# A decoder step's mixer: the scan's columns projected earlier, side steps priced in VectorE time, four raw weight buffers

## Chip, cores and metric

The kernel runs on one core of a Trainium2 chip. The metric is device time in microseconds (us) of one execution; the time before is the median of three runs. The profile is that of one further execution, and its own time stands in the table below.

## The reference

One layer of a decoder step for 256 prompt tokens, 16 learned meta tokens and 8 x 4 sample tokens, all in float32, model width 2048:

```
x = x + 1/2 * SwiGLU_1(rms(x))
[u_a | u_b | g_a | g_b] = rms(x) @ W_in
a = PoolMix(u_a)          # causal means over 2, 4, 8, 16 tokens, minus identity,
                          # a 256x256 map per group, a scale per channel
b = GLU(gelu(S5(u_b)))    # diagonal complex recurrence, 64 groups of 64 states
x = x + (sig(g_a) * (a @ W_a) + sig(g_b) * (b @ W_b)) @ W_out
x = x + 1/2 * SwiGLU_2(rms(x))
y = rms(x)
```

The last pooling inputs and the final S5 states are outputs too.

## The kernel before

Tokens are columns: 304 of them (`NT`) up to the mixer's first half, 288 (`NL`) once the meta tokens are dropped. Channels are partitions, in tiles of 128. Every product is made of three matmuls, because a float32 operand is split into a high and a low part in the faster type `fp32r`: high by high, high by low, low by high (`mm3`, lines 249 to 254).

All weights come in chunks of 512 x 256 in one fixed order, `weight_order`. For each chunk the load queue of SyncE fetches `raw` (L138), ScalarE casts its high part `whi` (L161) and VectorE subtracts to get the low part `wlo` (L172). There are `RAW = 3` raw buffers, and `AHEAD + 2 = 4` each for the two parts.

`proj` multiplies one chunk in 24 matmuls and then calls `step`. A `step` makes the high part of a later chunk, flushes `g.post` (work that reads finished PSUM banks), makes the low part, starts a load, and then takes some side steps: `g.owed` grows by `g.rate`, and for each whole unit one item is drawn from the generator `g.side`. All engines run their instructions in the order in which this program issues them, so the rate decides how much side work stands between two weight splits on VectorE.

Before the mixer the side work is the preparation of the S5 tables (`ssm_setup`, at `SETRATE`). In the mixer it is the pooling (`Pool.run`, at `POOLRATE = 3.5` items a step) and then the scan (`Scan.run`, at `MIXRATE = 1.53` items a step).

The mixer goes through these stages. First the eight column pairs of `W_in` for the two branches, in the order `COLS = (0, 1, 2, 4, 3, 5, 6, 7)`: 0 to 3 feed the pool, 4 to 7 the scan. Pair 0 is projected ahead of the mixer, while the norm's scale is still being worked out. Then come the pool's group maps (`mixed`), the eight pairs of the first gate with `w_branch_a` (6 steps each), the eight pairs of the second gate (4 steps each), the GLU, `w_branch_b` and `w_out`.

The scan has eight matrices `i`, each in two halves. One half is eight `rows` on VectorE (L965, L966, L949 with L951, two scans L955, L971, L959, L962). Between the rows the generator issues, at hand-written places: `into` (matmuls `bu` for the next matrix, copied by ScalarE), `outof` (24 matmuls `yps` for the matrix before, two rows into the next one), the pieces of `act` (gelu, on ScalarE and VectorE in turn), and the transfers of GpSimd's queue: `load` (`ee` from `esc`), `stored` and `stacked` (an input split, written to `usc` and read back as `us`), and `matrices` (`bs`, `cs`). `Scan.first` and `Scan.begin` do this for the first matrix, around and within the projection of pair 5. Before the scan's generator starts, `drain` issues all that is left of the pool.

The names that the change touches: `RAW`, `MIXRATE`, `POOLRATE`, `COLS`, `LAG`, `MIXLAG`; `step`, `also`, `drain`; `Scan.input`, `stored`, `into`, `outof`, `rows`, `run`; `Pool.run`, `means`; `mixer`.

Of the kernel before, what the change touches and what calls it, by code (L numbers as in the profile page):

```python
# [33 lines left out]
AHEAD = 2  # L34
RAW = 3
SETRATE = 1.25
MIXRATE = 1.53
WP = 1024
# [8 lines left out]
NCON = NT + NTV + 2  # L47
POOLRATE = 3.5
LATE = 8
STIR = 7  # L50
LAG = 0
MIXLAG = 2
COLS = (0, 1, 2, 4, 3, 5, 6, 7)
MAGIC = 12582912.0
# [128 lines left out]
def setup(ctx, tc, I):  # L183
    g = Ctx()
    nc = tc.nc
    g.tc, g.nc, g.I = tc, nc, I
    g.uid = 0
    g.side, g.rate, g.owed, g.post = None, 0, 0.0, []
    g.dram = ctx.enter_context(tc.tile_pool(name="dram", bufs=1, space=DRAM))
    g.const = ctx.enter_context(tc.tile_pool(name="const", bufs=1))  # L190
    g.w = Weights(g, ctx.enter_context(tc.tile_pool(name="wpool", bufs=2)))
    g.act = ctx.enter_context(tc.tile_pool(name="act", bufs=1))
    g.parts = {"X": (g.act, 2 * KD)}
    g.psum = ctx.enter_context(tc.tile_pool(name="psum", bufs=4, space=PSUM))
    g.psaux = ctx.enter_context(tc.tile_pool(name="psaux", bufs=3, space=PSUM))
    g.pslong = ctx.enter_context(tc.tile_pool(name="pslong", bufs=1, space=PSUM))
    g.downs = 0

    g.ones = g.const.tile([P, P], F32, name="ones")
    nc.vector.memset(g.ones, 1.0)  # L200
    g.vec = g.const.tile([P, NVEC], F32, name="vec")
    return g
# [17 lines left out]
def step(g):  # L220

    g.w.high()
    flush(g)
    g.w.low()
    g.w.load()
    g.owed += g.rate
    while g.owed >= 1.0:
        g.owed -= 1.0
        got = next(g.side, None) if g.side is not None else None
        if got is None:  # L230
            g.side = None

# [7 lines left out]
def also(g, more):  # L240
    g.side = more if g.side is None else chain(g.side, more)


def drain(g):
    while g.side is not None:
        if next(g.side, None) is None:
            g.side = None

# [590 lines left out]


class Scan:

# [8 lines left out]
    def input(self, ps, r):  # L851

        u = self.sp.tile([P, NT], F32, name=nm(self.g, "u"))
        self.g.nc.vector.tensor_tensor(u, ps, r, ALU.mult)
        self.u.append(u)
        if len(self.u) == 1:
            self.stored(0)
            self.stacked(0)
# [17 lines left out]
    def stored(self, i):  # L876

        g, nc = self.g, self.g.nc
        hi = self.sp.tile([P, NT], F32R, tag="uhi", name=nm(g, "uhi"), bufs=1)
        lo = self.sp.tile([P, NT], F32R, tag="ulo", name=nm(g, "ulo"), bufs=1)  # L880
        nc.scalar.copy(hi, self.u[i])
        nc.vector.tensor_tensor(lo, self.u[i], hi.bitcast(F32), ALU.subtract)
        for k, u in enumerate((hi, lo)):
            nc.gpsimd.dma_start(g.usc[i][k], u)
# [8 lines left out]
    def into(self, i, pair, ri, half, long=False):  # L893

        g = self.g
        if "row" not in pair[half]:
            pair[half]["row"] = self.sp.tile([P, 3, JB, NT], F32, tag="row", name=nm(g, "row"), bufs=4)
        row = pair[half]["row"][:, 1 + ri]
        for jj in range(JB):
            q = half * JB + jj  # L900
            ps = bank(g, "bu", aux=True, pool=g.pslong if long and jj else None)[:, :NT]
            g.nc.tensor.matmul(ps, self.bs[i][:, q, ri * P:(ri + 1) * P], self.up[:, q], start=True, stop=True)  # L902
            g.nc.scalar.copy(row[:, jj], ps)

    def outof(self, i, pair):
# [3 lines left out]
        c = self.cs[i].rearrange("p i (q c) -> p i q c", c=32)  # L909
        for k, h in enumerate((2, 1, 0)):  # L910
            for half, s in enumerate(pair):
                for jj in range(JB):
                    q = half * JB + jj
                    g.nc.tensor.matmul(self.yps[i][q * 32:q * 32 + 32], c[:, h, q], s["row"][:, h, jj, NMETA:],  # L914
                                       start=k == 0, stop=k == 2)

# [16 lines left out]
    def rows(self, sb, s):  # L933
# [23 lines left out]
        def back():  # L957
            x, e = (y.rearrange("p k j t -> p (k j) t")[:, :, NMETA:] for y in (row, ee))
            tt(x, x, e, ALU.mult)  # L959

        def states():
            tt(self.st[:, :, :, js].rearrange("p r k j -> p r j k"), both(one[:, :, S0 - 1::NS]),  # L962
               two[:, :, :, S0 - 1::NS], ALU.subtract)

        return [lambda: tt(fl(one), fl(two[:, 0]), fl(two[:, 1]), ALU.add),  # L965
                lambda: tt(row.rearrange("p k j t -> p (k j t)"), row.rearrange("p k j t -> p (k j t)"),  # L966
                           ee.rearrange("p k j t -> p (k j t)"), ALU.mult),
                turned,
                lambda: scan(2),
                lambda: scan(1),  # L970
                lambda: tt(one[:, :, NMETA:], two[:, 1, :, NMETA:], two[:, 0, :, NMETA:], ALU.add),  # L971
                back,
                states]

# [17 lines left out]
    def run(self):  # L992
# [4 lines left out]
        for i in range(KW):  # L997
            nxt = [{} for _ in range(half)]
            for h in range(half):
                sb = i * half + h  # L1000
                rows = self.rows(sb, pair[h])
                if sb >= 1 and sb + 1 < nb:
                    new = self.load(sb + 1)
                    (nxt[0] if h else pair[1])["ee"] = new["ee"]
                for n, row in enumerate(rows):
                    row()
                    if h == 0 and n == 2 and done is not None:
                        self.outof(i - 1, done)
                        acts = self.act(i - 1)
                    if h == 0 and n == 5 and i + 1 < KW:  # L1010
                        self.matrices(i + 1, ins=False)
                    k, late = divmod(h * len(rows) + n - 4, 3)
                    if i + 1 < KW and late == 0 and 0 <= k < 4:
                        self.into(i + 1, nxt, 1 - k % 2, k // 2)
                    if h == 0 and n == 1 and i + 2 < KW:
                        self.stored(i + 2)
                    if h and n == 6 and i + 2 < KW:
                        self.stacked(i + 2)
                        self.matrices(i + 2, outs=False)
                    while acts and h * len(rows) + n >= acts[0][0]:  # L1020
                        acts.pop(0)[1]()
                    yield 1
            done, pair = pair, nxt
        for _ in range(3):
            yield 1
        self.outof(KW - 1, done)
        yield 1
        for n, f in self.act(KW - 1):
            f()
            if n in (5, 7):  # L1030
                yield 1

# [5 lines left out]
class Pool:  # L1038


    def __init__(self, g, O):
# [9 lines left out]
        t2 = T()  # L1051
        self.f = [cut(t2, 0), cut(t2, 1)]
        self.LE = LE

# [3 lines left out]
    def run(self, p, pss, norm, out):  # L1058
# [6 lines left out]
        for u, end in zip(self.u, e):  # L1065
            nc.scalar.copy(end[:, :, HIST:], u[:, S0:].rearrange("p (b s) -> p b s", s=NS))
        yield 1
        for f in range(2):
# [4 lines left out]
    def means(self, w, u, e, out):  # L1073
# [4 lines left out]
        while k < w:  # L1078
# [3 lines left out]
            s, es, k, a = s2, e2, 2 * k, a ^ 1  # L1082
            yield 1
        stt(d[:, :NPR], s[:, NMETA:S0], 1.0 / w, u[:, NMETA:S0], ALU.mult, ALU.subtract)
        stt(d[:, NPR:].rearrange("p (b s) -> p b s", s=NS), es[:, :, HIST:], 1.0 / w, e[:, :, HIST:],
            ALU.mult, ALU.subtract)
        yield 1
        out.append(split(g, d, NL, "Y"))
        yield 1

# [7 lines left out]
def mixer(g, norm, O, ps0):  # L1098
# [8 lines left out]
    def gate(ps, c):  # L1107
        z = Z()[:, :NL]
        nc.vector.tensor_tensor(z, ps, norm.r[:, NMETA:], ALU.mult)
        nc.scalar.activation(z, z, AF.Sigmoid, bias=vcol(g, "b_gate", c))  # L1110
        return z

    with ExitStack() as cm:
        g.mix = cm.enter_context(g.tc.tile_pool(name="mix", bufs=1))
        with ExitStack() as cs:
# [3 lines left out]
            dparts, aparts = [], []  # L1119
            g.side, g.rate = None, POOLRATE  # L1120
            def spare(c):
                if c == KD // KC - 1:
                    g.owed -= MIXLAG

            for p in COLS:
                if p < KW // 2:
                    pool.fetch(p)
                before = {KW // 2 + 1: scan.begin, KW - 1: spare}.get(p)
                ps = proj(g, "w_in", p * 256, norm.x, NT, KD, before) if p else ps0
# [3 lines left out]
                else:  # L1133
                    g.post += [lambda q=q: scan.input(q, norm.r) for q in ps]
                if p == 1:
                    scan.first()
                if p == KW // 2 + 1:
                    drain(g)
                    g.side, g.rate = scan.run(), MIXRATE
                    g.owed = -LAG * MIXRATE  # L1140
            def mixed():
                g.owed -= MIXLAG
                for q in range(4):
# [4 lines left out]
                    for f in range(2):  # L1148
                        ps = bank(g, "pw")[:, :NL]
                        for k in range(2):  # L1150
# [3 lines left out]
                        g.post.append(lambda i=2 * q + f, ps=ps: aparts.append(  # L1154
                            split(g, ps, NL, "Y", vcol(g, "pool_scale", i))))
                    if q % 2:
                        step(g)

            mixed()
            for p in range(KD // 2):  # L1160
# [5 lines left out]
                def gated(p=p, z=z, pa=pa):  # L1166
                    for f in range(2):
                        nc.vector.tensor_tensor(z[f], pa[f], z[f], ALU.mult)
                        nc.sync.dma_start(msc[2 * p + f], z[f])

# [337 lines left out]
```

## Time and profile before

| what | value |
|---|---|
| median of three runs | 2317.06 us (2316.76 to 2318.68) |
| the profiled execution, its own time | 2318.77 us |
| its span, first to last instruction | 2316.8 us |
| granted TensorE clock, mean | 0.999 |
| mixer's first projection to the second gate's end | about 892 to 1285 us |
| weight traffic and all other DMA | 437.36 MB, mean 189 GB/s |

The span is what the engines' rows cover; some 2 us of the execution's time lie around it. Engines are named PE (TensorE matmul), PEld (its weight load), DVE (VectorE), ACT (ScalarE), POOL (GpSimd) and SP (SyncE). A row such as `wlo<-raw,whi` names the tile written and the tiles read, and `L172` the line of the kernel. Matmuls are pipelined: each is shown as about 0.3 us long while a new one starts every 0.13 to 0.14 us, so the count of matmuls in a stretch says more than the busy time.

### The profile page before, as it was taken

To read this page: it belongs to the slowest core of one execution; us is meant where nothing else is said; L and a number is where in the kernel's file an instruction comes from. 1 tells how busy PE (TensorE), PEld (TensorE's weight loads), DVE (VectorE), ACT (ScalarE), POOL (GpSimd) and SP (SyncE) were. 2 spreads that over 40 slices of the span, in tenths; PEclk is the share of its full clock that TensorE was granted. 3 is DMA by queue.
4 is the path that set the end of the run, shared out by engine and by line. 5 is a ranking of instruction groups with operands and counts; after the bars stand their busy time and mean duration, and the time that the engine had idled before them with its cause. 6 is when DMAs were issued, how large, how long until landed. Compare 5 with 4: busy or idle time off the path is not lost.

```text
span 2316.8 us, 41582 instructions
## 1 busy us (share of the span) xinstructions
PE 2306.3 (100%) x17073; PEld 2293.3 (99%) x17073; DVE 1576.1 (68%) x2303; ACT 942.9 (41%) x1316; POOL 134.8 (6%) x255
## 2 busy tenths in 40 slices
PE   9999999999999999999999999999999999999998
PEld 9999999999999999999999999999999999999998
DVE  7788777877654557799999765545555555555556
ACT  5333333343333335454444544433333333333333
POOL 0000000002200002211110130000000000000001
PEclk9999999999999999999999999999999999999999
DMA  6445555556654446767785775444444444444543
GB/s 230 160 151 188 197 209 205 189 202 212 203 174 160 156 155 214 238 220 246 258 265 199 235 264 175 163 167 162 172 164 166 167 168 164 164 165 166 169 159 128
DMA packets 133454, 437.36 MB, mean 189 GB/s; under 512 B 22064, under 2 KB 33632, under 8 KB 133136
## 3 DMA queue, kind: packets, MB, share of 16 engines
q1 hardware_dynamic: 107088, 375.51, 47.6%
q0 software_dynamic: 25792, 58.87, 8.4%
q8 instruction: 134, 2.20, 0.4%
q14 instruction: 56, 0.46, 0.1%
q10 hardware_dynamic: 384, 0.32, 0.0%
HBM read 403.07 MB, written 31.55 MB: 188 GB/s over the span
## 4 chain that ended last, share of the span: by engine, by line
PE 98%; DVE 1%; issue 0%; ACT 0%; DMA 0%; SPq 0%; ACTq 0%; DVEq 0%
PE pj L253 24%; PE pj L252 24%; PE pj L254 24%; PE dn L254 8%; PE dn L252 8%; PE dn L253 8%; PE yps L914 1%; PE bu L902 0%; DMA pk<-in_first 0%; PE o L1245 0%; DVE row L955 0%; DVE wlo L172 0%; PE pw L253 0%; PE pw L252 0%; PE pw L254 0%
## 5 line engine op out<-in xcount | busy, mean ns | idle before, releaser
L172 DVE TENSOR_TENSOR wlo<-raw,whi 128x1024 fp32r<-128x1024 f32 (+1 forms) x697 | 849.6, 1220 | 576.5 <-ACT whi L161 575.6
L161 ACT CAST whi<-raw 128x1024 fp32r<-128x1024 f32 (+1 forms) x697 | 729.1, 1048 | 1202.6 <-PE pj L253 690.7
L252 PE MATMUL pj<-X,whi 128*128 128x304 f32 (+1 forms) x2428 | 728.3, 300 | 0.7 <-ACT whi L151 0.7
L253 PE MATMUL pj<-X,whi 128*128 128x304 f32 (+1 forms) x2428 | 728.2, 300 | 0.0
L254 PE MATMUL pj<-X,wlo 128*128 128x304 f32 (+1 forms) x2428 | 727.8, 300 | 0.0
L253 PE MATMUL pj<-Y,whi 128*128 128x288 f32 x1728 | 510.6, 296 | 0.0
L252 PE MATMUL pj<-Y,whi 128*128 128x288 f32 x1728 | 509.4, 295 | 0.0
L254 PE MATMUL pj<-Y,wlo 128*128 128x288 f32 x1728 | 508.8, 294 | 0.0
L252 PEld LDWEIGHTS pj<-X,whi 128*128 128x128 f32 x2428 | 457.2, 188 | 4.0 <-issue 2.1
L253 PEld LDWEIGHTS pj<-X,whi 128*128 128x128 f32 x2428 | 456.6, 188 | 0.1
L254 PEld LDWEIGHTS pj<-X,wlo 128*128 128x128 f32 x2428 | 456.3, 188 | 0.2
L252 PEld LDWEIGHTS pj<-Y,whi 128*128 128x128 f32 x1728 | 325.1, 188 | 0.9 <-issue 0.5
L253 PEld LDWEIGHTS pj<-Y,whi 128*128 128x128 f32 x1728 | 324.9, 188 | 0.0
L254 PEld LDWEIGHTS pj<-Y,wlo 128*128 128x128 f32 x1728 | 324.6, 188 | 0.0
L254 PE MATMUL dn<-H,wlo 128*128 128x304 f32 x704 | 213.0, 303 | 0.0
L252 PE MATMUL dn<-H,whi 128*128 128x304 f32 x704 | 212.8, 302 | 0.0
L253 PE MATMUL dn<-H,whi 128*128 128x304 f32 x704 | 212.2, 301 | 0.0
L254 PE MATMUL dn<-X,wlo 128*128 128x288 f32 x688 | 203.0, 295 | 0.0
L253 PE MATMUL dn<-X,whi 128*128 128x288 f32 x688 | 203.0, 295 | 0.0
L252 PE MATMUL dn<-X,whi 128*128 128x288 f32 x688 | 202.7, 295 | 0.0
L253 PEld LDWEIGHTS dn<-H,whi 128*128 128x128 f32 x704 | 132.4, 188 | 0.0
L252 PEld LDWEIGHTS dn<-H,whi 128*128 128x128 f32 x704 | 132.3, 188 | 0.0
(278 smaller groups left out, 1816.5 us busy)
## 6 DMA issues: line engine op xcount, KB each, us to landing
raw<-in_ffn_w_gate SPq DMA_DIRECT2D x175, 512.0 KB, 3.3
raw<-in_ffn_w_up SPq DMA_DIRECT2D x175, 512.0 KB, 3.3
raw<-in_ffn_w_down SPq DMA_DIRECT2D x168, 512.0 KB, 3.3
raw<-in_w_in SPq DMA_DIRECT2D x96, 512.0 KB, 4.3
raw<-in_w_out SPq DMA_DIRECT2D x32, 512.0 KB, 3.9
esc<-ee POOLq DMA_DIRECT2D x16, 912.0 KB, 5.7
ee<-esc POOLq DMA_DIRECT2D x16, 912.0 KB, 5.9
raw<-in_w_branch_a SPq DMA_DIRECT2D x16, 512.0 KB, 4.2
```

The lines of the kernel that those rows point to most:

```text
L161: self.g.nc.scalar.copy(hi[:, :kn], self.raw[i][:, :kn])
L172: self.g.nc.vector.tensor_tensor(lo[:, :kn], raw[:, :kn], hi[:, :kn].bitcast(F32), ALU.subtract)
L252: mm(ps, wh, x[0], start=start, stop=False)
L253: mm(ps, wh, x[1], start=False, stop=False)
L254: mm(ps, wl, x[0], start=False, stop=stop)
L914: g.nc.tensor.matmul(self.yps[i][q * 32:q * 32 + 32], c[:, h, q], s["row"][:, h, jj, NMETA:], start=k == 0, stop=k == 2)
```

## The change

There are three parts.

The order: pairs 4 and 5, the scan's first, are projected second and fourth. The scan's generator starts after pair 5 as before, but without draining the pool: the pool now has a lane of its own, `g.front`, which is served ahead of `g.side`. The pool's result tiles are claimed when it is set up.

The pace: an item of a generator is no longer one unit. It yields VectorE's time for it in us, and `step` books that against `g.rate`, which is the time of a step (3.355 us with 304 columns, 3.186 with 288) less that of a weight split (1.135). Work that is issued outside the generators is booked too: inputs, gates and pool maps reduce `g.owed`, and the scan's own matmuls add to it, since they lengthen the step. The places of `into` in the row order are written as a list, and are the same as before. The switch `DIRECT` is empty, so the code that it chooses isn't used.

The buffers: `RAW` goes from 3 to 4.

```diff
-RAW = 3
+RAW = 4
 SETRATE = 1.25
-MIXRATE = 1.53
+LOWUS, SHORTUS, LONGUS = 1.135, 3.186, 3.355
+TIGHT = 0.0
...
-POOLRATE = 3.5
+DIRECT = ()
...
-COLS = (0, 1, 2, 4, 3, 5, 6, 7)
+COLS = (0, 4, 1, 5, 2, 3, 6, 7)
@@ def step
     g.owed += g.rate
     while g.owed >= 1.0:
-        g.owed -= 1.0
-        got = next(g.side, None) if g.side is not None else None
-        if got is None:
-            g.side = None
+        cost = ahead(g)
+        if cost is None:
+            g.owed = min(g.owed, 1.0)
+            break
+        g.owed -= cost
+
+
+def ahead(g):
+    for lane in ("front", "side"):
+        gen = getattr(g, lane)
+        cost = next(gen, None) if gen is not None else None
+        if cost is not None:
+            return cost
+        setattr(g, lane, None)
@@ def also
-    g.side = more if g.side is None else chain(g.side, more)
+    g.front = more if g.front is None else chain(g.front, more)
+INTO = (4, 7, 10, 13)
+VIEWED = (5, 7, 9)
@@ Scan.input, after the multiplication
+        self.g.owed -= 0.38
@@ Scan.stored, after the subtraction
+        g.owed -= 0.39
@@ Scan.into, for each matmul
+            g.owed += 0.14
@@ Scan.outof
+        used = (2, 1) if i in DIRECT else (2, 1, 0)
+        g.owed += 0.54 * len(used)
@@ Scan.rows
+        last = (1.33, direct) if sb * JB // 4 in DIRECT else (0.14, states)
+        return [(0.70, lambda: tt(fl(one), fl(two[:, 0]), fl(two[:, 1]), ALU.add)),
+                (1.97, lambda: tt(row.rearrange("p k j t -> p (k j t)"), row.rearrange("p k j t -> p (k j t)"),
+                                  ee.rearrange("p k j t -> p (k j t)"), ALU.mult)),
+                (1.59, turned),
+                (1.335, lambda: scan(2)),
+                (1.335, lambda: scan(1)),
+                (0.70, lambda: tt(one[:, :, NMETA:], two[:, 1, :, NMETA:], two[:, 0, :, NMETA:], ALU.add)),
+                (1.88, back),
+                last]
@@ Scan.run
                     while acts and at >= acts[0][0]:
-                        acts.pop(0)[1]()
-                    yield 1
+                        n, f = acts.pop(0)
+                        f()
+                        cost += 0.0 if n in VIEWED else 0.39
+                    yield cost
             done, pair = pair, nxt
-        for _ in range(3):
-            yield 1
+        for _ in range(2):
+            yield 2.0
         self.outof(KW - 1, done)
-        yield 1
+        yield 1.5
@@ Pool
+        self.parts = [(part(g, "Y", NL), part(g, "Y", NL)) for _ in range(KW)]
@@ Pool.run and Pool.means: 0.77 for the inputs, 0.55 a level, 0.45 the means, 0.37 the split
-        yield 1
+        yield 0.55
...
-        out.append(split(g, d, NL, "Y"))
-        yield 1
+        hi, lo = self.parts[len(out)]
+        g.nc.scalar.copy(hi, d)
+        tt(lo, d, hi.bitcast(F32), ALU.subtract)
+        out.append((hi, lo))
+        yield 0.37
@@ mixer
-            g.side, g.rate = None, POOLRATE
+            g.side, g.rate = None, LONGUS - LOWUS
...
-                before = {KW // 2 + 1: scan.begin, KW - 1: spare}.get(p)
+                before = scan.begin if p == KW // 2 + 1 else None
...
-                if p == 1:
+                if p == KW // 2:
                     scan.first()
                 if p == KW // 2 + 1:
-                    drain(g)
-                    g.side, g.rate = scan.run(), MIXRATE
-                    g.owed = -LAG * MIXRATE
+                    g.side, g.owed = scan.run(), 0.0
+            g.rate = SHORTUS - LOWUS - TIGHT
             def mixed():
-                g.owed -= MIXLAG
...
+                        g.owed -= 0.40
@@ gate, and the product with w_branch_a
+        g.owed -= 0.37
```

More of the change, by code (lines that the diff above doesn't have):

```diff
@@ L47 @@
 NCON = NT + NTV + 2
-POOLRATE = 3.5
+DIRECT = ()
 LATE = 8
 STIR = 7
-LAG = 0
-MIXLAG = 2
-COLS = (0, 1, 2, 4, 3, 5, 6, 7)
+COLS = (0, 4, 1, 5, 2, 3, 6, 7)
 MAGIC = 12582912.0
@@ L187, in setup @@
     g.uid = 0
-    g.side, g.rate, g.owed, g.post = None, 0, 0.0, []
+    g.front, g.side, g.rate, g.owed, g.post = None, None, 0, 0.0, []
     g.dram = ctx.enter_context(tc.tile_pool(name="dram", bufs=1, space=DRAM))
@@ L240, in also @@
 def also(g, more):
-    g.side = more if g.side is None else chain(g.side, more)
+    g.front = more if g.front is None else chain(g.front, more)
 def drain(g):
-    while g.side is not None:
-        if next(g.side, None) is None:
-            g.side = None
+    while ahead(g) is not None:
+        pass
 def mm3(g, ps, wh, wl, x, start, stop):
@@ L909, in outof @@
         c = self.cs[i].rearrange("p i (q c) -> p i q c", c=32)
-        for k, h in enumerate((2, 1, 0)):
+        used = (2, 1) if i in DIRECT else (2, 1, 0)
+        g.owed += 0.54 * len(used)
+        for k, h in enumerate(used):
             for half, s in enumerate(pair):
@@ L914, in outof @@
                     g.nc.tensor.matmul(self.yps[i][q * 32:q * 32 + 32], c[:, h, q], s["row"][:, h, jj, NMETA:],
-                                       start=k == 0, stop=k == 2)
+                                       start=k == 0, stop=k == len(used) - 1)
     def act(self, i):
@@ L959, in back, with direct @@
             tt(x, x, e, ALU.mult)
+        st = self.st[:, :, :, js].rearrange("p r k j -> p r j k")
         def states():
[L962 to L973, printed above, removed]
+            tt(st, both(one[:, :, S0 - 1::NS]), two[:, :, :, S0 - 1::NS], ALU.subtract)
+        def direct():
+            x = two[:, :, :, NMETA:]
+            tt(x, x, both(one[:, :, NMETA:]), ALU.subtract)
+            nc.scalar.activation(st, two[:, :, :, S0 - 1::NS], AF.Copy, scale=-1.0)
+        last = (1.33, direct) if sb * JB // 4 in DIRECT else (0.14, states)
[8 more added lines that the diff above has]
+                last]
     def first(self):
@@ L1004, in run @@
                     (nxt[0] if h else pair[1])["ee"] = new["ee"]
-                for n, row in enumerate(rows):
+                for n, (cost, row) in enumerate(rows):
                     row()
-                    if h == 0 and n == 2 and done is not None:
+                    at = h * len(rows) + n
+                    if at == 2 and done is not None:
                         self.outof(i - 1, done)
                         acts = self.act(i - 1)
-                    if h == 0 and n == 5 and i + 1 < KW:
+                    if at == 5 and i + 1 < KW:
                         self.matrices(i + 1, ins=False)
-                    k, late = divmod(h * len(rows) + n - 4, 3)
-                    if i + 1 < KW and late == 0 and 0 <= k < 4:
+                    if i + 1 < KW and at in INTO:
+                        k = INTO.index(at)
                         self.into(i + 1, nxt, 1 - k % 2, k // 2)
-                    if h == 0 and n == 1 and i + 2 < KW:
+                    if at == 1 and i + 2 < KW:
                         self.stored(i + 2)
-                    if h and n == 6 and i + 2 < KW:
+                    if at == 14 and i + 2 < KW:
                         self.stacked(i + 2)
                         self.matrices(i + 2, outs=False)
-                    while acts and h * len(rows) + n >= acts[0][0]:
-                        acts.pop(0)[1]()
-                    yield 1
+                    while acts and at >= acts[0][0]:
+                        n, f = acts.pop(0)
+                        f()
+                        cost += 0.0 if n in VIEWED else 0.39
+                    yield cost
             done, pair = pair, nxt
-        for _ in range(3):
-            yield 1
+        for _ in range(2):
+            yield 2.0
         self.outof(KW - 1, done)
-        yield 1
+        yield 1.5
         for n, f in self.act(KW - 1):
             f()
-            if n in (5, 7):
-                yield 1
+            if n in VIEWED[:2]:
+                yield 1.5
     def store(self, O):
@@ L1066, in run @@
             nc.scalar.copy(end[:, :, HIST:], u[:, S0:].rearrange("p (b s) -> p b s", s=NS))
-        yield 1
+        yield 0.77
         for f in range(2):
@@ L1082, in means @@
             s, es, k, a = s2, e2, 2 * k, a ^ 1
-            yield 1
+            yield 0.55
         stt(d[:, :NPR], s[:, NMETA:S0], 1.0 / w, u[:, NMETA:S0], ALU.mult, ALU.subtract)
@@ L1086, in means @@
             ALU.mult, ALU.subtract)
-        yield 1
-        out.append(split(g, d, NL, "Y"))
-        yield 1
+        yield 0.45
+        hi, lo = self.parts[len(out)]
[3 more added lines that the diff above has]
+        yield 0.37
     def keep(self, p):
@@ L1119, in mixer @@
             dparts, aparts = [], []
-            g.side, g.rate = None, POOLRATE
-            def spare(c):
-                if c == KD // KC - 1:
-                    g.owed -= MIXLAG
+            g.side, g.rate = None, LONGUS - LOWUS
             for p in COLS:
@@ L1134, in mixer @@
                     g.post += [lambda q=q: scan.input(q, norm.r) for q in ps]
-                if p == 1:
+                if p == KW // 2:
                     scan.first()
                 if p == KW // 2 + 1:
-                    drain(g)
-                    g.side, g.rate = scan.run(), MIXRATE
-                    g.owed = -LAG * MIXRATE
+                    g.side, g.owed = scan.run(), 0.0
+            g.rate = SHORTUS - LOWUS - TIGHT
             def mixed():
-                g.owed -= MIXLAG
                 for q in range(4):
@@ L1168, in gated @@
                         nc.vector.tensor_tensor(z[f], pa[f], z[f], ALU.mult)
+                        g.owed -= 0.37
                         nc.sync.dma_start(msc[2 * p + f], z[f])
```

## The prediction

> **What bounds the kernel now.** I read the page's busy times first, then busy time by stretch, then who waits for whom, and last the chain of work in the one place where the chain leaves TensorE.
>
> ```profile
> span 2316.8 us, 41582 instructions
> PE 2306.3 (100%) x17073; PEld 2293.3 (99%) x17073; DVE 1576.1 (68%) x2303; ACT 942.9 (41%) x1316; POOL 134.8 (6%) x255
> L161 ACT CAST whi<-raw 128x1024 fp32r<-128x1024 f32 (+1 forms) x697 | 729.1, 1048 | 1202.6 <-PE pj L253 690.7
> ```
>
> TensorE is busy for 2306.3 of 2316.8 us, and its weight loads for nearly as long. VectorE has a third of the span free, but not everywhere. Busy time of pipelined matmuls could still hide a loose cadence, so the counts by stretch come next (columns: stretch, its length, then busy us and instructions of PE, PEld, DVE, ACT and POOL, granted clock, DMA share, GB/s):
>
> ```profile
> 150.00:200.00 50.00, 50.00 (x360) 50.00 (x359) 39.76 (x62) 18.97 (x23) 0.00 (x0) 1.00 0.44 149
> 700.00:750.00 50.00, 50.00 (x360) 50.00 (x359) 23.99 (x30) 17.96 (x21) 0.00 (x0) 1.00 0.47 159
> 1500.00:1550.00 50.00, 50.00 (x379) 50.00 (x378) 25.98 (x32) 19.00 (x24) 0.00 (x0) 1.00 0.49 167
> 1028.00:1240.00 212.00, 211.95 (x1661) 205.41 (x1662) 203.63 (x230) 103.49 (x174) 29.35 (x56) 1.00 0.78 247
> 2305.00:2317.00 12.00, 3.95 (x27) 2.42 (x25) 6.32 (x17) 5.09 (x14) 3.42 (x2) 0.83 0.51 197
> ```
>
> With 304 columns a matmul starts every 50/360 us = 138.9 ns, at 39.76 us of VectorE work beside it as at 23.99; with 288 columns every 50/379 us = 131.9 ns. A step of the projection loop is 24 matmuls (4 slices, 2 halves, 3 products), so a long step lasts 3.333 us and a short one 3.166. The mixer's scan, about 1028 to 1240, is the only stretch in which another engine is as full: VectorE 203.63 of 212 us, or 96%. Of the few things that TensorE waited for in the whole execution, one lies in the mixer (us in total, times, longest):
>
> ```profile
> PE yps L914 <- DVE row L959: 0.5, 1, 0.5
> ```
>
> The matmuls `yps`, which read the finished scan, wait 0.5 us for VectorE's multiplication `row` of line 959. The chain of work there (start, us, what):
>
> ```profile
> 1241.91 1.88 DVE row L959
> 1243.83 1.65 PE yps L914 x20
> ...
> 1280.59 1.59 PE yps L914 x24
> ```
>
> The chain leaves TensorE, runs through VectorE's row and comes back at 1243.83. So VectorE fell behind until TensorE felt it, once, and the last scan result was projected at 1280.59. The change orders VectorE's work; it can give back only what TensorE lost there. The number of matmuls, their shapes and their clock stay.
>
> **The change, part by part.** *Side steps paced by VectorE's time.* Each step now owes VectorE the time of a short step less a weight split (3.186 - 1.135 = 2.05 us; long 3.355 - 1.135 = 2.22), and each side step pays its own price. The prices against VectorE's timeline (start, duration; I take start to next start, since durations overlap by some 0.08):
>
> ```profile
> 1100.50 2.05 DVE L966 TENSOR_TENSOR row<-row,ee 128x1824 f32<-128x1824 f32 x1
> 1102.47 0.47 DVE L882 TENSOR_TENSOR ulo<-u,uhi 128x304 fp32r<-128x304 f32 x1
> 1102.85 1.42 DVE L949 TENSOR_TENSOR row<-row 128x1216 f32<-128x1216 f32 x1
> 1104.30 0.22 DVE L951 TENSOR_TENSOR row<-row,ah 128x32 f32<-128x32 f32 x1
> 1104.44 1.22 DVE L172 TENSOR_TENSOR wlo<-raw,whi 128x1024 fp32r<-128x1024 f32 x1
> 1105.57 1.42 DVE L955 TENSOR_TENSOR_SCAN row<-d,row 128x608 f32<-128x608 f32 x1
> 1106.91 1.20 DVE L172 TENSOR_TENSOR wlo<-raw,whi 128x1024 fp32r<-128x1024 f32 x1
> ...
> 1109.36 0.49 DVE L925 SCALAR_TENSOR_TENSOR gy<-u,vec,yps 128x288 f32<-128x288 f32 x1
> 1109.76 0.75 DVE L971 TENSOR_TENSOR row<-row 128x576 f32<-128x576 f32 x1
> 1110.43 0.82 DVE L1109 TENSOR_TENSOR z<-pj,rs_y 128x288 f32<-128x288 f32 x2
> ...
> 1112.44 1.95 DVE L959 TENSOR_TENSOR row<-row,ee 128x1728 f32<-128x1728 f32 x1
> 1114.31 0.45 DVE L927 SCALAR_TENSOR_TENSOR gw<-gw,gy 128x288 f32<-128x288 f32 x1
> 1115.81 0.22 DVE L962 TENSOR_TENSOR states<-row 128x36 f32<-128x36 f32 x1
> 1115.94 0.79 DVE L965 TENSOR_TENSOR row<-row 128x608 f32<-128x608 f32 x1
> ```
>
> Line 966 takes 1.97 us (price 1.97), lines 949 and 951 together 1.59 (1.59), a scan 1.34 (1.335), line 971 0.67 (0.70), line 959 1.87 (1.88), line 962 0.13 (0.14); a weight split 1.13 (1.135); a small one, as lines 882 and 925, 0.38 to 0.40 (0.39). These rows of one half, with a second scan, cost 8.91 us against 8.95 booked (line 965 aside). So the prices are right to half a per cent. The step is booked a little long: 3.186 against 3.166, 3.355 against 3.333, so 0.02 us more VectorE work per step than TensorE gives time for.
>
> *The order.* The pair of columns 4 and 5 comes second and fourth instead of fourth and sixth. The scan's first row (now after six projections) can start after four, two long projections or 8 x 3.333 = 26.7 us earlier; the pool steps of pairs 2 and 3 go ahead of it in their lane and cost, by the booked prices, 5.7 + 6.8 = 12.5 us. Budget of the 16 long steps left after it starts: 16 x 2.22 = 35.5, less 12.5 and six inputs at 0.38, is 20.7 us; the pool matmuls add 0.9; 48 short steps of the first gate 48 x 2.05 less 32 gate operations at 0.37 is 86.6. One of the eight scan matrices costs 2 x 9.65 + 4 x 0.39 + 0.39 = 21.25, less 2.74 credited for its own matmuls: 18.5. So 108.2/18.5 = 5.85 of 8 are through after the first gate, and the rest, 40 us at 2.05 - 0.185 per step, takes 21 of the second gate's 32 steps. Before, the scan filled that stage to its end. I expect the last `yps` some 20 to 30 us before 1280.59. Nothing waits for it then, so the earlier end by itself gives nothing.
>
> *Four raw buffers.* Waits between 1083 and 1243 (ScalarE's longest, the load queue's, VectorE's), and two VectorE waits between 930 and 1028:
>
> ```profile
> ACT whi L161 <- DMA raw<-in_w_in: 20.2, 9, 6.8
> SPq L138 <- DVE wlo L172: 105.3, 40, 4.8
> DVE wlo L172 <- ACT whi L161: 4.4, 6, 1.3
> DVE Y L278 <- ACT Y L277: 2.0, 4, 0.5
> DVE Y L281 <- ACT Y L280: 1.9, 4, 0.8
> ```
>
> A ring closes here: a load waits for VectorE's split of the chunk three ahead of it (105.3 us), ScalarE waits for the load (20.2 us), and VectorE for ScalarE (4.4 us in 160, or 0.09 a step). With a fourth buffer the load waits for the split before that one and may leave a step, 3.17 us, earlier. I cost the edit at nothing on TensorE; it takes most of 0.09 us a step off VectorE.
>
> The page's row of those loads:
>
> ```profile
> raw<-in_w_in SPq DMA_DIRECT2D x96, 512.0 KB, 4.3
> ```
>
> They land in 4.3 us. The Trainium skill's "DMA: Bandwidth & Descriptors", section "Issuing engines are not separate DMA queues", says that transfers from all queues run on the same 16 engines and interleave, which speaks against more loads in flight: stretched by four thirds to 5.7 us, an estimate from the row, a load would still land 1.8 us earlier than now, and the sum stays.
>
> *The rest.* `DIRECT` is empty, so `direct` is never issued; the pool's result tiles are claimed earlier, not filled earlier; `ahead` chooses between lanes when the kernel is built. These issue no instruction and cost nothing. Pair 4's inputs need the scale that the first pool step finishes; that step stays two steps behind the first projection, and the inputs come three steps after it, so no wait is added there.
>
> *Sum.* How far may VectorE lag? A chunk's high part overwrites that of the fourth chunk before it, so its split can end at most three short steps less a cast (1.05) and a split (1.13) ahead of need: 9.5 - 2.2 = 7.3 us. Booked 87 steps (16 long, 2, 48, 21) at 0.02 cost 1.8 us of it; the ACT handovers that no price holds (all of line 281's 1.9 us, half of line 278's 2.0) cost 2.9. That is 4.7 of 7.3, if the fourth buffer removes the 0.09 a step. So the stall of 0.5 us goes, and nothing else can go, since no other wait of TensorE lies in the mixer. I take -0.5 us: 2318.77 (the profiled execution: the span of 2316.8 and 2.0 around it) becomes 2318.3, and the median of the runs, which lies 1.7 below that execution at 2317.06, becomes **2316.6**.
>
> **The rivals.** *No gain.* The booked load (99.6% of a step and more) leaves VectorE as late as now, and `yps` or a split costs 0.5 to 1 us at another place. For it speaks that the load per step rises slightly and that 4.7 of 7.3 us are spent; against it the fourth buffer. Time 2317.1.
>
> *VectorE overbooked: slower.* If the waits of VectorE on ScalarE stay at 4.4 in 160 us, the 300 us of the new, longer full stretch lose 8.3; with 1.8 of overbooking that is 10.1, 2.8 over the lead of 7.3, and with the 2.9 of handovers 5.7 over. TensorE then idles a little in every step near the end of the first gate. Time 2316.6 + 2.8 to 2316.6 + 5.7: 2319.4 to 2322.3. It decides from a loss of 0.084 us a step (7.3/87) on. Against it: the waits come from the raw loads by the rows above, and an engine that lags finds its inputs ready. The row 2305 to 2317 shows what idling can add: 3.95 us busy of 12 at a clock of 0.83. The Trainium skill's "TensorE: Matmul & The Clock Gate", Part 1, says that an idle window of about 3.4 us halves the clock for as long again; dribbled stalls of 0.1 us would not trip it, one stall of that size would add about 1.7 us, an estimate from that page.
>
> *The first inputs late.* The change puts the two loads of `ee` directly ahead of the transfers that feed the first `bu` matmuls. Rows: two landing times between 900 and 1010, the issue of the `us` loads, and their use.
>
> ```profile
> ee<-esc POOLq DMA_DIRECT2D x3, 912.0 KB, 9.2
> us<-usc POOLq DMA_DIRECT2D x6, 152.0 KB, 4.6
> 952.02 1.64 POOL L891 DMA_DIRECT2D us<-usc  x3 [1.94 <-DMA usc<-uhi]
> 963.35 0.72 PE L902 MATMUL bu<-us,bs 96*128 96x304 f32 x4
> ```
>
> Now `us` lands about 952.0 + 1.6 + 4.6 = 958.2, 5.1 us ahead of its use, with one projection between, as after the change. If it also queues behind the two `ee` loads for their 9.2 us, it is late by 9.2 - 5.1 = 4 us at worst; since GpSimd can issue them before the pair's projection has been read, I take 3: 2319.6.
>
> *A looser cadence gained.* If matmuls were slowed by VectorE's traffic, moving it would speed them. Counts of 360 at 39.76 and at 23.99 us bound this to 1 in 360, over the stage's 340 us 0.9 us: 2315.7.
>
> **How the numbers follow.** Chances: forecast 0.62, no gain 0.18, overbooked 0.12, late inputs 0.05, cadence 0.03. The predicted time is 2316.6. The range runs from 2315.0 (the cadence case less 0.7 for the scatter of runs, whose lowest is 2316.76 and highest 2318.68) to 2320.8 (the middle of the overbooked case), which leaves out the upper half of that case and unseen causes. A measurement of this kernel can tell about 0.2%, 4.6 us, from no change. Faster by that much would need TensorE idle time that isn't there: 0.02. Slower takes the upper end of the overbooked case and one long stall: 0.07. Within: 0.91.
>
> **What would show it.** Right: TensorE's waits have no mixer row of over 0.5 us; VectorE's first row of line 965 stands near 950; the last `yps` between 1250 and 1262; ScalarE's wait for `raw` in the scan falls from 20.2 us to under 7, and VectorE's for `whi` with it. Wrong: a row "PE pj <- DVE wlo" of several us, a `yps` or `bu` wait of over 1 us, or a span under 2313 with the same matmul count.

## The result, and the profile after

The changed kernel takes 2329.99 us, median of four runs (2327.65 to 2330.45), against 2317.11 us for the kernel before, measured beside it. The ratio is 1.0052 with a 95% interval of 1.0035 to 1.0070: slower by some 12.9 us, where 2316.6 was forecast. The profiled execution took 2330.45 us, with a span of 2328.6.

First the page's busy times, and then what TensorE waited for, longest first (us in total, times, longest; of the rows left out none is over 1.0 us, and none lies in the mixer):

```profile
span 2328.6 us, 41576 instructions
PE 2310.6 (99%) x17073; PEld 2298.2 (99%) x17073; DVE 1577.9 (68%) x2303; ACT 942.6 (40%) x1316; POOL 134.9 (6%) x255
```

```profile
PE pw L260 <- DVE u L866: 5.1, 1, 5.1
PE bu L916 <- DMA usc<-uhi: 3.3, 1, 3.3
...
PE pj L260 <- DVE z L1140: 0.3, 1, 0.3
```

The same 17073 matmuls are there. The wait of `yps` is gone, as forecast, and two new ones have come: the pool maps' matmuls `pw` wait 5.1 us for VectorE, and the first `bu` matmuls wait 3.3 us for a transfer. That is 8.4 us, and the span has grown by 11.8. The rest shows in the stretches right behind the two waits (columns as before; the granted clock is the third number from the end):

```profile
939.50:946.60 7.10, 7.08 (x30) 7.10 (x31) 3.63 (x10) 2.73 (x6) 0.00 (x0) 0.55 0.48 164
1015.00:1021.00 6.00, 5.93 (x25) 5.93 (x26) 3.84 (x8) 1.51 (x3) 0.46 (x1) 0.50 0.53 187
946.60:952.00 5.40, 5.40 (x41) 5.40 (x40) 2.26 (x4) 3.68 (x7) 3.71 (x7) 1.00 0.78 154
```

After each wait the clock is granted at about half for some 6 us. Behind the first, 30 matmuls take 7.10 us where 30 x 138.9 ns = 4.2 would do: 2.9 us more. Behind the second, 25 take 6.0 us instead of 25 x 131.9 ns = 3.3: 2.7 more. So the first stall costs 3.3 + 2.9 = 6.2 us and the second 5.1 + 2.7 = 7.8; with the 0.5 us gained at `yps` the mixer should be 13.5 us longer. Between the norm sums ahead of and behind it (before at 908.89 and 1479.11, after at 908.35 and 1492.21) it is 13.6 longer. The remaining difference to the span, 1.8 us the other way, lies outside the mixer: 0.5 us ahead of it, where the kernel before with four raw buffers (run e4 below) is 0.4 us earlier too, and 1.3 us behind it. The cause of the latter wasn't tested.

How the first stall comes about, in GpSimd's timeline:

```profile
914.71 1.07 POOL L1125 DMA_DIRECT2D out<-pt  x2 [15.54 <-DVE pt L1092]
...
919.68 1.06 POOL L876 DMA_DIRECT2D ee<-esc  x2
920.73 0.55 POOL L1084 DMA_DIRECT2D pt<-in_state_pool  x1
922.83 0.54 POOL L898 DMA_DIRECT2D usc<-uhi  x1 [1.54 <-ACT uhi L894]
923.36 0.54 POOL L898 DMA_DIRECT2D usc<-ulo  x1
934.04 0.56 POOL L905 DMA_DIRECT2D us<-usc  x1 [10.14 <-DMA usc<-uhi]
```

The two `ee` loads leave 3 us ahead of `usc`. The small write, which landed in 2.6 us (median between 900 and 1010) in the kernel before, now takes over 10, and `us` can only be read back when it has landed. The chain of work shows that wait (start, us, what):

```profile
923.36 11.84 DMA usc<-ulo
935.49 0.43 POOL us L905
...
939.52 1.35 PE bu L916 x4
```

The profile infers who released whom: its row names `usc` for the wait of `bu`, but what these matmuls read is `us`, whose last read is issued at 936.03 and lands 2.9 us later.

And the second stall, in VectorE's timeline:

```profile
1008.22 1.96 DVE L976 TENSOR_TENSOR row<-row,ee 128x1728 f32<-128x1728 f32 x1
1010.10 1.22 DVE L171 TENSOR_TENSOR wlo<-raw,whi 128x1024 fp32r<-128x1024 f32 x1
1011.23 0.22 DVE L981 TENSOR_TENSOR states<-row 128x36 f32<-128x36 f32 x1
1011.37 0.78 DVE L989 TENSOR_TENSOR row<-row 128x608 f32<-128x608 f32 x1
1012.19 2.06 DVE L990 TENSOR_TENSOR row<-row,ee 128x1824 f32<-128x1824 f32 x1
1014.16 0.47 DVE L895 TENSOR_TENSOR ulo<-u,uhi 128x304 fp32r<-128x304 f32 x1
1014.55 0.85 DVE L866 TENSOR_TENSOR u<-pj,rs_y 128x304 f32<-128x304 f32 x2
```

The second pair of `pw` results takes over the PSUM banks of pair 7's projection, whose sums VectorE must read first (`u`, L866). TensorE is ready for them at about 1010; VectorE works through scan rows until 1014.55. Nothing else on TensorE could go ahead, since its order is fixed.

Two things went as forecast: the scan starts earlier and ends earlier. The last `yps`, 1280.59 before, in the chain:

```profile
1271.28 1.59 PE yps L931 x24
```

With 13.6 us of added stalls taken off, it would stand at 1257.7, 23 us earlier.

### The profile page after: what moved, and what is told of

The parts are those of the page before. It is cut to its first block, busy times and chain, and to the rows that moved or that the text cites. A ratio compares the mean times of both kernels' runs of the same rounds, so it can differ in the third digit from the quotient of the medians.

```text
span 2328.6 us, 41576 instructions
## 1 busy us (share of the span) xinstructions
PE 2310.6 (99%) x17073; PEld 2298.2 (99%) x17073; DVE 1577.9 (68%) x2303; ACT 942.6 (40%) x1316; POOL 134.9 (6%) x255
## 4 chain that ended last, share of the span: by engine, by line
PE 97%; DVE 1%; DMA 1%; issue 1%; POOL 0%; ACT 0%; DVEq 0%; ACTq 0%; POOLq 0%
PE pj L260 24%; PE pj L261 24%; PE pj L262 23%; PE dn L262 8%; PE dn L260 8%; PE dn L261 8%; PE yps L931 1%; DMA usc<-ulo 1%; PE bu L916 0%; DVE wlo L171 0%; PE o L1273 0%; DMA pk<-in_first 0%; PE pj L456 0%; DMA usc<-uhi 0%; PE pw L260 0%
```

## The experiments

The question after the comparison: are these two local stalls, each with its own cause, or does one VectorE booked to the brim surface in two places and go on surfacing wherever it is let go?

**e1_us_ahead.** The first two `ee` loads are issued behind the first input's transfers.

```diff
@@ Scan.first
         self.matrices(0)
-        self.pair = [self.load(0), self.load(1)]
@@ Scan.input, first input
             self.stored(0)
             self.stacked(0)
+            self.pair = [self.load(0), self.load(1)]
```

> The changed kernel with one move: the two ee loads of the first scan matrix are issued behind the transfers usc and us of the first input instead of ahead of them. Two-stall theory: the bu wait of 3.3 us and the slow restart behind it go, 6.4 us in all, so about 2323.6; the pool maps' wait of 5.1 us stays. Overbooked-VectorE theory: the bu wait goes, but VectorE loses the rest it had there and waits of several us come up later; 2327 to 2330.

Measured: 2322.83 us (ratio to the kernel before 1.0023, 1.0014 to 1.0032), 7.2 less than the changed kernel. In GpSimd's timeline the reads of `us` now start 8 us earlier:

```profile
926.12 0.56 POOL L906 DMA_DIRECT2D us<-usc  x1 [3.08 <-DMA usc<-uhi]
```

No `bu` wait is left, and the `pw` wait stays at 5.1 us. So far this fits the two-stall theory.

**e2_reserve.** VectorE time is kept free ahead of the pool maps.

```diff
+            def spare(c):
+                if c == 2:
+                    g.owed -= 5.2
...
-                before = scan.begin if p == KW // 2 + 1 else None
+                before = {KW // 2 + 1: scan.begin, KW - 1: spare}.get(p)
```

> The changed kernel with one line: 5.2 us of VectorE time are kept free in the last half of pair 7's projection, ahead of the pool's maps (as the kernel before kept two items free). Two-stall theory: the pw wait of 5.1 us and its slow restart go, 7.8 us in all, so about 2322; the bu wait stays. Overbooked-VectorE theory: the lag only shows later, as waits of yps or of weight splits in the gates; 2327 to 2330.

Measured: 2323.68 us (1.0027, 1.0015 to 1.0038), 6.3 less. The `pw` wait is gone; the `bu` wait stays at 2.9 us, and the wait of the first gate's matmuls for VectorE's `z` has grown from 0.3 to 1.1 us. So the second stall goes, and a tenth of its 7.8 us returns later: the overbooking is there, but small. The time is 1.7 us above what was expected, in six executions from 2322.48 to 2326.08.

**e3_both.** Both edits.

> Both edits in the changed kernel. Two-stall theory: 2330.0 less 6.4 and 7.8, so 2315.8, within 0.1% of the kernel before (2317.1), and no wait of TensorE over 1 us in the mixer. Overbooked-VectorE theory: 2320 or more, with new waits of TensorE on VectorE in the gates.

Measured: 2318.33 us (1.0002, 0.9994 to 1.0011). The two parts nearly add up: 7.2 + 6.3 = 13.5 against 11.7 together. In the traces the slow stretch behind the stall that was left is shorter than in the changed kernel, by 0.6 us in e1 and 1.3 in e2 (last section); together that is as large as the 1.8 us between 13.5 and 11.7. What is left of TensorE's mixer waits is one row:

```profile
PE pj L260 <- DVE z L1140: 1.1, 1, 1.1
```

The time is 2.5 us above what was expected; of that the trace names only the wait of 1.1 us.

**e4_old_raw4.** The kernel before with `RAW = 4`.

> The kernel before with four raw buffers and nothing else. If the fourth buffer is harmless: 2316.5 to 2317.5, ScalarE's waits for raw in the scan (20.2 us between 1083 and 1243) fall below 7 us, and the yps wait of 0.5 us goes. If it does harm by more loads in flight (the GpSimd queue's transfers land later): a bu wait of over 1 us, 2319 or more.

Measured: 2316.64 us (0.9996, 0.9987 to 1.0005). The fourth buffer does no harm in the old order. The `yps` wait is gone, and between the two norm sums the trace is 1.4 us shorter than that of the kernel before (568.79 against 570.22). The waits of ScalarE and VectorE in the scan, between 1083 and 1243:

```profile
ACT whi L161 <- DMA raw<-in_w_in: 16.5, 9, 5.0
DVE wlo L172 <- ACT whi L161: 3.5, 5, 1.3
```

The first row fell only from 20.2 to 16.5 us, where under 7 was expected: with VectorE this late, one step more of lead on the loads takes a fifth of that wait away, not most of it.

**e5_fill.** In the changed kernel, 24 matmuls whose result nobody reads stand ahead of the first `bu`.

```diff
+FILL = 24
...
+        if c == 1:
+            x = self.x0
+            ps = bank(self.g, "fill", aux=True)[:, :NT]
+            for n in range(FILL):
+                self.g.nc.tensor.matmul(ps, x[:, :P], x, start=n == 0, stop=n == FILL - 1)
...
+            scan.x0 = norm.x[0][0]
```

> The changed kernel with 24 more matmuls of 304 columns (their result is read by nobody) issued just ahead of the first bu matmuls, so that TensorE works where it waited 3.3 us. If the slow matmuls behind the wait come from the idle time: the wait and the slow restart of some 3 us both go, the added work costs its 3.3 us in the wait's place, 2330.0 less 3 is about 2327, and matmuls after it start every 139 ns. If the clock drops for another reason (the transfers, VectorE's load): no gain, 2330 or more.

Measured: 2327.04 us (1.0043, 1.0027 to 1.0059), 3.0 less than the changed kernel, with 24 matmuls more. The four executions scatter from 2326.09 to 2329.82, so the trace is the better witness. TensorE's rows there:

```profile
935.79 3.47 PE L1014 MATMUL fill<-X 128*128 128x304 f32 x24
939.11 0.77 PE L917 MATMUL bu<-us,bs 96*128 96x304 f32 x4
943.10 0.71 PE L917 MATMUL bu<-us,bs 96*128 96x304 f32 x4
```

The `bu` matmuls start about as late as in the changed kernel (939.1 against 939.5), and those behind them run at full speed: the next 24 take from 939.7 to 943.1, 141 ns each. So the second half of the stall's price is a matter of idleness: it goes when the time is filled with useless work.

**e6_old_first_late.** The kernel before, with `scan.first()` behind pair 4's projection, as in the changed kernel.

```diff
-                if p == 1:
+                if p == KW // 2:
                     scan.first()
```

> The kernel before, old order, with one edit: Scan.first (matrices and the two ee loads) is called behind pair 4's projection instead of pair 1's, so that the ee loads stand directly ahead of usc and us as in the changed kernel. If that place is the cause of the first stall by itself: a bu wait of 2 to 4 us and a slow restart, 2317.4 + 5 to 7, about 2323. If it takes the new order too (the pool's transfers, an earlier VectorE load): no bu wait, 2317 to 2318.

Measured: 2318.22 us (1.0001, 0.9992 to 1.0010) and no `bu` wait. The place in the program isn't the cause by itself. GpSimd's timeline shows why:

```profile
939.93 0.58 POOL L863 DMA_DIRECT2D ee<-esc  x1
941.20 0.54 POOL L863 DMA_DIRECT2D ee<-esc  x1 [0.68 <-DMA out<-pt]
948.34 0.54 POOL L884 DMA_DIRECT2D usc<-uhi  x1 [5.60 <-ACT uhi L881]
```

GpSimd runs ahead of the projection and issues the loads 7 to 8 us ahead of `usc`. In the changed kernel it can't: pair 4 comes second, and until 914.71 the queue is held by the pool's first outputs (15.54 us idle, by its row above), which wait for VectorE's first pool step and so for the norm's scale. Only there do the `ee` loads come 3 us ahead of `usc`.

**e7_old_no_reserve.** The kernel before with `MIXLAG = 0`.

> The kernel before with MIXLAG 0 instead of 2: no items are kept free ahead of and within the pool's maps. If the missing reserve alone makes the second stall: a pw wait of 1 to 5 us, 2319 to 2324. If it takes VectorE being full for the four pairs ahead of it, as the new order makes it: VectorE is still some 4 us ahead there in the old order, no pw wait, 2317 to 2318.

Measured: 2321.25 us (1.0016, 1.0007 to 1.0026), with this wait in the mixer, and two shorter ones, of 0.6 and 0.5 us, for VectorE in the first gate:

```profile
PE pw L252 <- DVE u L854: 1.7, 1, 1.7
```

So the reserve that the change drops is needed in the old order too; there its loss makes a wait of 1.7 us. The other 3.4 us of the 5.1 I put down to VectorE being booked in full over the four projections ahead in the new order, but no run isolates that, so it isn't shown.

**e8_both_tight.** Run e3 with 0.1 us less of VectorE booked per short step.

```diff
-TIGHT = 0.0
+TIGHT = 0.1
```

> Run e3_both with TIGHT 0.1: 0.1 us less of VectorE booked per short step. If the rest over the kernel before (2318.3 against 2317.4, and a wait of 1.1 us of pj for VectorE's z) is VectorE lag from booking the whole step: the wait goes and the time falls to 2316.5 to 2317.2. If it is not: no change, 2318.

Measured: 2316.40 us (0.9995, 0.9986 to 1.0004); no wait of TensorE lies in the mixer. That is 1.9 below e3, of which the wait of 1.1 us is the part that the trace names. It is the fastest version of this study beside e4, and it can't be told from the kernel before.

**e9_tight_raw3.** Run e8 with three raw buffers.

> Run e8_both_tight with three raw buffers again. If the fourth buffer carries part of the changed kernel's pace: ScalarE's wait for raw in the scan comes back to 20 us or more, VectorE's wait for whi with it, TensorE waits 1 us or more for VectorE again, 2317.5 to 2319. If the pace and the reserve do it alone: 2316.4, as with four.

Measured: 2318.41 us (1.0002, 0.9993 to 1.0010), with these rows of TensorE, and of ScalarE between 1083 and 1243:

```profile
PE pw L260 <- DVE u L866: 1.4, 1, 1.4
ACT whi L160 <- DMA raw<-in_w_in: 15.2, 10, 3.1
```

In e8 ScalarE's wait for `raw` in that stretch is a fifth of this:

```profile
ACT whi L160 <- DMA raw<-in_w_in: 3.2, 3, 1.7
```

With VectorE not late, the fourth buffer does what was expected of it on ScalarE (3.2 against 15.2 us), and less for VectorE's wait for `whi` in that stretch (4.5 against 5.2). With the whole step booked it does less: the same row is 10.5 us in e3, and in the changed kernel it reads

```profile
ACT whi L160 <- DMA raw<-in_w_in: 15.9, 5, 6.3
```

Whether the 2 us between e8 and e9 come from it can't be settled from these runs, whose intervals overlap; a `pw` wait of 1.4 us came back.

**e10_ee_act_queue.** In the changed kernel the first two `ee` loads are issued at the same place on ScalarE's queue instead of GpSimd's.

```diff
-        self.pair = [self.load(0), self.load(1)]
+        self.pair = [self.load(h, self.g.nc.scalar) for h in range(2)]
@@ Scan.load
-    def load(self, sb):
+    def load(self, sb, eng=None):
...
-        g.nc.gpsimd.dma_start(ee, g.esc[sb])
+        (eng or g.nc.gpsimd).dma_start(ee, g.esc[sb])
```

> The changed kernel with the first two ee loads at the same place but issued on ScalarE's queue instead of GpSimd's. If usc was late because it stood behind ee in the same queue: usc lands in 3 to 5 us instead of 11.8, the bu wait and its restart go, about 2323.5. If it was late because both share the same engines, whatever the queue: usc still takes 8 us or more, a bu wait of 1 to 3 us stays, 2327 to 2330.

Measured: 2330.44 us (1.0053, 1.0038 to 1.0069), no gain at all, and a `bu` wait of 5.0 us, longer than either theory had it. The stretch in which `usc` is under way, in the changed kernel and then here, with the DMA engines' share second from the end:

```profile
919.00:934.00 15.00, 15.00 (x110) 15.00 (x109) 7.64 (x9) 6.37 (x9) 3.35 (x7) 1.00 0.98 356
919.00:934.00 15.00, 15.00 (x110) 15.00 (x109) 8.67 (x11) 6.97 (x8) 3.08 (x7) 1.00 1.05 360
```

And the times from issue to landing, of the low part's write (issued between 922 and 924) and of the reads that follow it, first in the changed kernel, then here:

```profile
usc<-ulo POOLq DMA_DIRECT2D x1, 152.0 KB, 11.8
us<-usc POOLq DMA_DIRECT2D x3, 152.0 KB, 2.9
...
usc<-ulo POOLq DMA_DIRECT2D x1, 152.0 KB, 9.7
us<-usc POOLq DMA_DIRECT2D x3, 152.0 KB, 6.5
```

The queue alone was not the cause. Out of the queue of `ee` the write lands 2 us sooner, but still takes 9.7 us, and the reads take 3.6 us more. The 16 engines are full for 15 us whichever queue the bytes came from, and a small transfer that is issued behind the `ee` loads is late. The Trainium skill says so in "DMA: Bandwidth & Descriptors", section "Issuing engines are not separate DMA queues": transfers from all queues run on the same engines and interleave. Here the trace agrees, with the 9.7 us above. In e1 the engines are as full in this stretch (share 1.06), but there `usc` is issued ahead of `ee`, and lands in 3.9 us. So moving the loads in time helps; moving them to another queue doesn't. Whether the fourth raw buffer has a part in it wasn't run (the changed kernel with three); with three, the kernel before shows a share of 0.96 in the same stretch.

## Why the prediction was wrong

**The bound held.** TensorE bounds the kernel, the 17073 matmuls are the same, and little could be gained: the wait at `yps` went, and the best versions (e4, e8) lie 0.7 and 1.0 us below the kernel before, which their intervals can't tell from it.

**The prices held.** In the rows above line 976 takes 1.88 us from start to start and line 990 1.97, as booked. The scan's first row stands at 955.96, or 949.8 without the first stall's 6.2 us (forecast near 950), and its last `yps` at 1257.7 without the added stalls (forecast 1250 to 1262). Overbooking costs little: 1.1 us of waiting in e3, none with 0.1 us less per step.

**First failing step: a lead of 7.3 us for everything.** The sum measured VectorE's lag against the weight splits alone, which have four buffers, and kept 2.6 us over. It didn't ask what else TensorE waits for VectorE for. The pool maps need PSUM banks that VectorE must empty first, within half a step: there the lead is the 12 matmuls of the first pair of maps, 1.6 us at 131.9 ns each, not 7.3. The old kernel kept two items free at just that place, and the prediction counted the loss of that reserve nowhere. Why VectorE was late there is shown only in part. Its handovers with ScalarE aren't booked: of 29.1 us in the projections ahead, with every step booked in full, it is busy 25.8, and of the 3.3 us of idle time 2.0 are four waits of 0.5 us for ScalarE's half of a split. The sum had such handovers, at 2.9 us, but set them against the lead of 7.3.

```profile
973.50:1002.60 29.10, 29.10 (x211) 29.10 (x210) 25.80 (x55) 13.07 (x21) 2.14 (x4) 1.00 0.49 167
```

Keeping time free there (e2) gave 6.3 us back; with its restart this is the larger of the two stalls in the trace, 7.8 us.

**Second failing step: the rival with late inputs was given 0.05.** Its mechanism was named right, `usc` and `us` late behind `ee`, and its wait came out as sized (3 us forecast, 3.3 measured), in part by luck, since it was worked out from the place in the queue, and in another queue the wait is 5.0 (e10). Its chance was wrong: the 5.1 us of slack were read from the old order, in which the `ee` loads leave at 920.47 and `usc` only at 949.00; after the change 3 us lie between.

**Third: the price of a wait.** A wait was costed at its own length. Measured, the wait of 3.3 us costs 6.2, since TensorE runs at half speed for some 6 us afterwards; e5 showed that idleness causes it. So that rival's 2319.6 would have been some 3 us too low. The prediction drew the slow restart from the Trainium skill's "TensorE: Matmul & The Clock Gate", Part 1, but used it only for the overbooked rival, and at 1.7 us. The Trainium skill's idle window of about 3.4 us isn't a threshold for the length of a wait here: in e2 a wait of 2.9 us was enough.

**The fourth buffer** was costed at nothing on TensorE, which e4 confirms within its interval. ScalarE's wait for `raw` was to fall from 20.2 us to under 7 and fell to 15.9; VectorE's for `whi` fell from 4.4 to 1.9 us in the changed kernel and to 3.5 in e4.

Both stalls together, each with its restart, are the whole loss of the mixer: 6.2 + 7.8 - 0.5 against 13.6 us, and e3 without them is level with the kernel before.

## What to carry to other kernels

Where an engine is full, ask of every edge on which it waits how many buffers lie between, and take the smallest: a lead that four weight buffers allow says nothing about a PSUM bank that is needed again half a step later. When work is moved, look at what the DMA engines carry at the new time, not in which queue it stands. And cost a TensorE wait of some 3 us or more at more than its length, by 1.6 to 2.9 us in these runs, because of the slow matmuls behind it.

## What the runs showed of the hardware

The clock falls some time after the wait began, not with the first matmul behind it. In e2, after a wait of 2.93 us, TensorE runs at full speed for 1.5 us and only then slows down:

```profile
938.66 0.80 PE L916 MATMUL bu<-us,bs 96*128 96x304 f32 x4 [2.93 <-DMA usc<-uhi]
...
940.14 0.43 PE L260 MATMUL pj<-X,whi 128*128 128x304 f32 x1
940.37 0.46 PE L261 MATMUL pj<-X,whi 128*128 128x304 f32 x1
```

From 940.37 on a matmul starts every 0.25 us instead of every 0.139. A wait of 1.74 us (e7) left the clock at full:

```profile
1004.00:1012.00 8.00, 6.38 (x46) 6.13 (x47) 7.28 (x13) 5.77 (x11) 1.36 (x3) 1.00 0.23 86
```

Waits of up to 1.7 us cost their length in these runs, and those of 2.9 us and more cost more, by differing amounts. Here are the slow stretches behind the wait of 2.93 us in e2, and, in e1, the end of the wait of 5.1 us and the stretch behind it:

```profile
938.66:943.70 5.04, 5.04 (x25) 5.04 (x26) 1.79 (x4) 2.73 (x6) 0.00 (x0) 0.66 0.38 112
...
1005.60:1007.80 2.20, 0.00 (x0) 0.00 (x0) 2.20 (x4) 0.00 (x0) 0.14 (x1) 0.50 0.96 347
1007.80:1012.50 4.70, 4.70 (x20) 4.70 (x21) 2.58 (x6) 1.00 (x2) 0.39 (x1) 0.51 0.60 203
```

In e2 25 matmuls take 5.04 us instead of 3.47, 1.6 more; behind the 3.3 us of the changed kernel it was 2.9. In e1 20 matmuls take 4.70 us instead of 2.64, 2.1 more, where the same wait cost 2.7 more in the changed kernel: in e1 the clock had been at half for the last 2.2 us of the wait already, when no matmul ran. What decides when the clock falls wasn't tested.
